# Four feed-forward weight units: the low part by a VectorE subtraction in place of an accumulating load

## The chip, the cores and the metric

The kernel runs on one core of one Trainium2 chip. The metric is the device time of one execution in microseconds. Its engines are TensorE (PE; PEld is its weight load), VectorE (DVE), ScalarE (ACT), GpSimd (POOL) and SyncE (SP), which only issues transfers here.

## The reference

The reference is a trunk of two decoder layers on 512 positions of width 1024, in float32. Layer 0 mixes tokens with a gated linear recurrence (RG-LRU), layer 1 with gated linear attention; each mixer is followed by a gated feed-forward block with a causal convolution of width 3. Every block stands between two RMS norms, scaled, shifted and gated by columns that a matrix makes from a conditioning vector. Cut to what matters here:

```
def conv_ffn(h, w_up, conv_w, conv_b, w_down):
    u = causal_dwconv(h @ w_up, conv_w, conv_b)
    g, val = jnp.split(u, 2, axis=-1)
    return (jax.nn.gelu(g) * val) @ w_down
...
        x = x + gt_m * rmsnorm(y, norm_g[i, 1])
        h = rmsnorm(x, norm_g[i, 2]) * (1.0 + sc_f) + sh_f
        y = conv_ffn(h, ffn_w_up[i], ffn_conv_w[i], ffn_conv_b[i], ffn_w_down[i])
```

In layer 0, `y` ahead of these lines is the output projection of the recurrent block. The feed-forward width is 2816, so `w_up` is 1024 x 5632.

## The kernel before, in words

**Layout.** Features lie on the 128 partitions and positions along the free dimension: `x` is 8 tiles of 128x512. Every weight matrix is cut into units of eight 128x128 blocks, 512 KB each (`unit_list`, L37), laid out in DRAM in the order of use. `("up", 0, p)` is the unit that makes 128 gate columns of layer 0's feed-forward block, `("up", 0, 22 + p)` the matching value columns.

**Split products.** A float32 matrix product is made of three products in a faster format, fp32r: high by high, high by low, low by high (`mm3`, L607). So each weight has a high part, its value rounded to fp32r by an ACT copy, and a low part, the value less the high part.

**How a unit gets there.** `load_upto` (L557) loads a unit into one of 3 `raw` buffers (SP queue, L464). ACT copies it to the high part (L438). The low part comes in one of two ways. In the ordinary way DVE subtracts the high part from `raw` (L579 and L599, recorded at L386): it needs the load and the ACT copy. Where `BYLOAD` (L480) holds, ACT writes the negated high part (L576 and L596, recorded at L433), and POOL issues a second load of the same unit from DRAM that adds to it (L469); `raw` is then free once ACT has read it twice. Most units land in one of 8 `w` slots (2048 columns, both parts); the units of `GWU` (L486), for layer 0 the pairs 1, 2 and 3, land in four general tiles `g` of 512 columns each, the high and low of two halves.

**Who comes by load.** Before the change the predicate holds for the eight units `rgg` of the recurrent block's gate branch, and for units 0, 1, 22 and 23 of `up` in layer 0: the first two pairs. Of these four, 0 and 22 lie in `w` slots (one accumulating load of 512 KB each), 1 and 23 in `g` tiles (two of 256 KB each).

**Where they are used.** `out_proj` (L746) ends the recurrent block: products of 8 output tiles, for the first half of the positions (256 columns) and then for the second; in each half the sum of squares over features (a matmul with a column of ones into a `nr` bank), its power -1/2 on POOL (L388), a broadcast matmul, then per tile a multiplication by it, the addition to `x` (both DVE), the square (ACT) and the addition to the sum (DVE); that sum goes through PE again, and `h_tile` (L732) makes the input of the feed-forward block. While this goes on for the first half, PE works on the products of the second half. The feed-forward block starts with `proj_halves` (L839) on its first seven units, 0, 22, 1, 23, 2, 24 and 3: for the first half of the positions all seven at feature tiles 0 and 1, and then each through tiles 2 to 7.

**Who sets the order.** All instructions are first recorded and then ordered by a planner (`Sched.order`, L192), a simulation with costs for each operation. It fixes one order for each engine, SP's and POOL's queues among them, and the engines then run strictly in it. PE and SP take the ready operation that was recorded first, the others the one with the longest rest of the way; DVE may wait a little for a more urgent operation (L299). The planner prices a load at its bytes by 360 KB per us and some 2 us, on one DMA stream (L323), an accumulating load at its bytes by 180 KB per us, 1.5 us ahead and 3.5 us behind (L326). What takes longer on the chip than in the plan stops the engine whose next instruction waits for it.

Of the kernel before, what the change touches and what calls it, by code (L numbers as in the profile page):

```python
# [20 lines left out]
KF = FF // P  # L21
# [455 lines left out]
                   after=after)  # L477


BYLOAD = lambda what, *i: what == 'rgg' or what == 'up' and i[0] == 0 and i[1] % KF < 2  # L480
SQ_GROUPS = ((0, 1, 2, 3, 4, 5), (6, 7))
WARM = (5, 2)
FULL = (1, 2, 2, 4)
# [13 lines left out]
def trunk(ctx, tc, xT, wall, adaT, par_d, c_d, walpha_d, ident_d, masks_d, outT):  # L497
# [56 lines left out]

    byload = {j for j, (key, _, _) in enumerate(UNITS) if BYLOAD(*key)}

# [834 lines left out]
```

## Time and profile before

| | |
|---|---|
| median of 3 runs | 1178.27 us (1177.48 to 1179.84) |
| the profiled execution's own time | 1178.37 us |
| its span, first to last instruction | 1176.6 us |
| mean granted TensorE clock | 0.996 |
| busy: DVE, ACT, POOL | 72%, 47%, 3% of the span |
| DMA | 163.68 MB, mean 139 GB/s |

The profile is one execution. Its page gives the busy time of each engine, the queues, the chain of work that ended last, and the costliest groups of instructions; other views give instructions in order of time, what an engine's idle time was ended by, and the same sums for stretches of the span. All times inside the execution are counted from the span's start. Most instructions are recorded by helpers, so one line stands for many: L386 is every DVE operation on two tensors, L399 every DVE scalar-tensor-tensor, L433 every ACT activation, L438 every ACT copy, L458 every matmul. Tiles tell them apart: `w<-raw,w` is a unit's subtraction, `g<-raw,g` that of half a unit in general tiles, `gh` are tiles of one half of the positions.

### The profile page before, as it was taken

To read this page: it belongs to the slowest core of one execution; us is meant where nothing else is said; L and a number is where in the kernel's file an instruction comes from. 1 tells how busy PE (TensorE), PEld (TensorE's weight loads), DVE (VectorE), ACT (ScalarE), POOL (GpSimd) and SP (SyncE) were. 2 spreads that over 40 slices of the span, in tenths; PEclk is the share of its full clock that TensorE was granted. 3 is DMA by queue.
4 is the path that set the end of the run, shared out by engine and by line. 5 is a ranking of instruction groups with operands and counts; after the bars stand their busy time and mean duration, and the time that the engine had idled before them with its cause. 6 is when DMAs were issued, how large, how long until landed. Compare 5 with 4: busy or idle time off the path is not lost.

```text
span 1176.6 us, 16159 instructions
## 1 busy us (share of the span) xinstructions
PE 1155.1 (98%) x6271; PEld 994.7 (85%) x6271; DVE 852.5 (72%) x1415; ACT 555.2 (47%) x878; POOL 36.8 (3%) x51
## 2 busy tenths in 40 slices
PE   7999998999999999999999999999999999999998
PEld 5876888988888888889988888899988888888887
DVE  6999977986777888766968787549745556645635
ACT  4499765544323424443578445444644333424411
POOL 0110020000000000000100000000000000000000
PEclk9999998999999999999999999999999999999999
DMA  9888593566575577531332103213143333233202
GB/s 363 280 237 272 179 280 102 162 205 209 177 231 185 183 233 232 153 113 35 112 108 90 55 18 109 72 37 108 38 160 90 108 92 106 90 105 93 72 1 72
DMA packets 47150, 163.68 MB, mean 139 GB/s; under 512 B 5121, under 2 KB 7681, under 8 KB 47074
## 3 DMA queue, kind: packets, MB, share of 16 engines
q1 hardware_dynamic: 45058, 156.36, 40.1%
q0 software_dynamic: 2016, 6.29, 3.0%
q8 instruction: 49, 0.80, 0.3%
q14 instruction: 27, 0.22, 0.1%
HBM read 160.54 MB, written 2.10 MB: 138 GB/s over the span
## 4 chain that ended last, share of the span: by engine, by line
PE 82%; ACT 7%; DVE 6%; DMA 3%; issue 1%; POOL 0%; DVEq 0%; SPq 0%; ACTq 0%; POOLq 0%
PE mm L458 80%; ACT g L433 3%; DMA raw<-in_wall_dram 3%; PE nr L458 2%; DVE g L399 2%; ACT L433 1%; DVE w L399 1%; DVE g L386 1%; ACT w L438 1%; DVE gh L386 1%; ACT w L433 1%; DVE w L386 1%; ACT g L438 1%; DVE gh L399 1%; DVE const L386 0%
## 5 line engine op out<-in xcount | busy, mean ns | idle before, releaser
L458 PE MATMUL mm<-g,w 128*128 128x512 f32 (+1 forms) x4846 | 947.1, 356 | 1.9 <-DVE g L386 0.9
L458 PEld LDWEIGHTS mm<-g,w 128*128 128x128 f32 x4846 | 803.7, 189 | 131.3 <-DVE g L386 1.6
L438 ACT CAST w<-raw 128x1024 fp32r<-128x1024 f32 x178 | 186.0, 1047 | 216.0 <-PE mm L458 203.9
L386 DVE TENSOR_TENSOR w<-raw,w 128x1024 fp32r<-128x1024 f32 (+1 forms) x168 | 203.5, 1215 | 74.1 <-ACT w L438 73.2
L399 DVE SCALAR_TENSOR_TENSOR g<-mm,const,g 128x510 f32<-128x510 f32 (+3 forms) x199 | 146.8, 747 | 97.6 <-ACT g L433 88.1
L386 DVE TENSOR_TENSOR g<-g,g 128x512 f32<-128x512 f32 (+2 forms) x213 | 126.7, 612 | 28.1 <-ACT g L438 13.3
L433 ACT ACTIVATE g<-mm,const 128x512 f32<-128x512 f32 (+1 forms) x144 | 100.9, 704 | 15.4 <-PE mm L458 15.3
L433 ACT ACTIVATE g<-g 128x512 f32<-128x512 f32 (+1 forms) x132 | 66.7, 538 | 83.3 <-DVE g L399 66.7
L458 PE MATMUL mm<-g,g 128*128 128x256 f32 (+4 forms) x716 | 98.7, 293 | 0.0
L458 PEld LDWEIGHTS mm<-g,g 128*128 128x128 f32 (+1 forms) x716 | 91.4, 191 | 4.2
L438 ACT CAST g<-g 128x512 fp32r<-128x512 f32 (+1 forms) x71 | 42.8, 608 | 107.5 <-DVE g L386 106.7
L399 DVE SCALAR_TENSOR_TENSOR araw<-araw,const 128x1024 f32<-128x1024 f32 x72 | 86.3, 1219 | 3.9 <-DMA araw<-in_adaT_dram 3.8
L386 DVE TENSOR_TENSOR g<-g,mm 128x512 f32<-128x512 f32 (+1 forms) x74 | 44.4, 612 | 42.6 <-PE mm L458 42.1
L386 DVE TENSOR_TENSOR gh<-gh,gh 128x256 f32<-128x256 f32 x97 | 40.3, 421 | 31.5 <-ACT gh L433 29.6
L458 PE MATMUL mm<-w,g 128*128 128x512 f32 x192 | 46.5, 394 | 0.2 <-ACT g L438 0.2
L390 POOL TENSOR_TENSOR sm<-sm,const 128x2 f32<-128x2 f32 (+1 forms) x19 | 18.8, 990 | 886.9 <-DVE sm L410 873.4
L458 PEld LDWEIGHTS mm<-w,g 128*128 128x128 f32 x192 | 35.4, 188 | 7.5 <-ACT g L438 0.4
L433 ACT ACTIVATE gh<-g 128x256 f32<-128x256 f32 x32 | 12.6, 413 | 48.6 <-DVE g L386 48.6
L433 ACT ACTIVATE g<-gh,const 128x256 fp32r<-128x256 f32 x48 | 22.5, 505 | 24.7 <-DVE gh L399 24.0
L399 DVE SCALAR_TENSOR_TENSOR w<-w,const 128x1024 f32<-128x1024 f32 x24 | 28.6, 1218 | 0.0
L433 ACT ACTIVATE gh<-const 128x256 f32<-128x256 f32 x48 | 18.8, 414 | 19.5 <-DVE const L386 19.3
L438 ACT COPY g<-mm 128x512 f32<-128x512 f32 (+1 forms) x39 | 21.0, 555 | 14.1 <-PE mm L458 14.0
(80 smaller groups left out, 537.5 us busy)
## 6 DMA issues: line engine op xcount, KB each, us to landing
raw<-in_wall_dram SPq DMA_DIRECT2D x192, 512.0 KB, 3.7
araw<-in_adaT_dram SPq DMA_DIRECT2D x72, 512.0 KB, 4.6
w<-in_adaT_dram SPq DMA_DIRECT2D x24, 512.0 KB, 8.0
w<-in_wall_dram POOLq DMA_DIRECT2D x10, 512.0 KB, 7.4
const<-in_xT_dram SPq DMA_DIRECT2D x4, 512.0 KB, 5.1
out_dram<-const SPq DMA_DIRECT2D x8, 256.0 KB, 2.1
g<-in_wall_dram POOLq DMA_DIRECT2D x4, 256.0 KB, 9.4
araw<-in_masks_dram SPq DMA_DIRECT2D x1, 512.0 KB, 6.3
```

Of the source, the lines that this page charges most:

```text
L386: self.s.add(eng, dur, lambda: e.tensor_tensor(out.ap(), a.ap(), b.ap(), op=op), [a, b], [out])
L390: lambda: self.nc.gpsimd.tensor_tensor(out.ap(), a.ap(), b.ap(), op=ALU.pow), [a, b], [out])
L399: return self.nc.vector.scalar_tensor_tensor(out.ap(), a.ap(), f(sc), b.ap(), op0=op0, op1=op1, **kw)
L433: return self.nc.scalar.activation(out.ap(), a.ap(), func, **kw)
L438: self.s.add("act", (0.095 if self._sb(a) else 0.052) + out.n * 0.8325e-3, lambda: self.nc.scalar.copy(out.ap(), a.ap()), [a], [out], afte ...
L458: r.append(self.nc.tensor.matmul(g[0].ap(), g[1].ap(), g[2].ap(), start=g[3], stop=g[4], **kw))
```

## The change

The predicate that names the units with accumulating loads loses its second part:

```
-BYLOAD = lambda what, *i: what == 'rgg' or what == 'up' and i[0] == 0 and i[1] % KF < 2
+BYLOAD = lambda what, *i: what == 'rgg'
```

The eight units of the gate branch are loaded as before. Units 0, 22, 1 and 23 of layer 0's feed-forward block now go through `e.tt(..., ALU.subtract)` at L579 and L599, as all other units do. The negating ACT copies and the accumulating loads of these four are not recorded any more, and the planner orders the whole program anew.

## The prediction

> **What bounds the kernel now.** I began with the page: its first lines and the DMA issues (count, KB each, us from issue to landing).
>
> ```profile
> span 1176.6 us, 16159 instructions
> PE 1155.1 (98%) x6271; PEld 994.7 (85%) x6271; DVE 852.5 (72%) x1415; ACT 555.2 (47%) x878; POOL 36.8 (3%) x51
> raw<-in_wall_dram SPq DMA_DIRECT2D x192, 512.0 KB, 3.7
> w<-in_wall_dram POOLq DMA_DIRECT2D x10, 512.0 KB, 7.4
> g<-in_wall_dram POOLq DMA_DIRECT2D x4, 256.0 KB, 9.4
> ```
>
> PE is busy for 1155.1 of 1176.6 us, so only 21.5 us can be won without taking PE work away. The ten `w` loads on POOL are the eight gate units and units 0 and 22; the four `g` loads are the halves of units 1 and 23. So 6 of 14 accumulating loads go. Next, whom PE waits for in the whole span (total, times, longest), and the chain that ended last (start, us), around the longest of these waits and after it:
>
> ```profile
> PE nr L458 <- DVE gh L386: 5.9, 1, 5.9
> PE nr L458 <- POOL sm L390: 0.6, 2, 0.3
> ```
>
> ```profile
> 163.45 14.04 DMA raw<-in_wall_dram
> 179.00 0.44 DVE gh L386
> 179.57 0.98 PE nr L458 x4
> 180.56 3.41 PE mm L458 x15
> 183.97 0.78 PE nr L458 x4
> 194.82 0.40 PE nr L458 x4
> 195.22 1.90 PE mm L458 x15
> 197.12 0.44 PE nr L458 x4
> 206.20 0.34 PE nr L458 x4
> ```
>
> ```profile
> 208.88 331.53 PE mm L458 x1632
> ```
>
> The largest wait of PE, 5.9 us, is for the first half's sum in the recurrent block's output projection, and the chain goes back from it to a raw load of 14.04 us. From 208.88 on PE has work for 331.53 us without a break, so what is won here reaches the end. Whom that wait goes back to is seen in the engines' timelines, ACT first, then DVE (the bracket is the idle time ahead):
>
> ```profile
> 168.55 0.63 ACT L433 ACTIVATE g<-raw 128x512 fp32r<-128x512 f32 x1 [2.88 <-DMA raw<-in_wall_dram]
> 177.51 1.14 ACT L438 CAST g<-raw 128x512 fp32r<-128x512 f32 x2 [2.94 <-DMA raw<-in_wall_dram]
> ```
>
> ```profile
> 165.09 0.75 DVE L386 TENSOR_TENSOR gh<-g,nr 128x256 f32<-128x256 f32 x2 [2.54 <-PE nr L458]
> 170.78 0.42 DVE L386 TENSOR_TENSOR gh<-gh,gh 128x256 f32<-128x256 f32 x1 [2.60 <-ACT gh L433]
> 179.00 1.22 DVE L386 TENSOR_TENSOR gh<-gh,gh 128x256 f32<-128x256 f32 x3 [3.45 <-ACT gh L433]
> ```
>
> ACT stands twice at the head of its queue with an instruction on a raw tile that has not landed (2.88 and 2.94 us). The squares of `x` for the norm are queued behind, and DVE, which adds them up, idles 2.60 and 3.45 us. Without these 6.05 us the sum would have been ready at 179.57 - 6.05 = 173.52. The stretches show that PE's work ran out then (columns: stretch, busy time and instructions of PE, PEld, DVE, ACT and POOL, granted clock, DMA share, GB/s):
>
> ```profile
> 156.00:165.00 9.00, 9.00 (x78) 9.00 (x77) 5.06 (x13) 7.08 (x15) 3.36 (x4) 1.00 0.78 223
> 165.00:173.68 8.68, 8.68 (x73) 8.48 (x71) 5.99 (x18) 5.80 (x16) 1.78 (x3) 1.00 1.06 277
> 173.68:179.57 5.89, 0.00 (x1) 0.03 (x1) 2.44 (x8) 2.96 (x8) 0.81 (x1) 0.84 0.79 195
> 179.57:184.75 5.18, 5.18 (x25) 5.18 (x26) 3.41 (x8) 0.55 (x2) 0.83 (x1) 0.52 0.63 176
> 184.75:197.57 12.82, 12.82 (x109) 12.82 (x109) 10.88 (x26) 7.89 (x18) 0.87 (x1) 1.00 0.18 57
> 197.57:209.00 11.43, 11.43 (x98) 11.43 (x98) 10.53 (x28) 4.91 (x11) 1.07 (x1) 1.00 0.36 124
> ```
>
> PE is idle from 173.68 to 179.57, and after that runs at 0.52 of its clock until 184.75. In the chain the same 4, 15 and 4 matmuls take 0.98, 3.41 and 0.78 us there and 0.40, 1.90 and 0.44 in the second half: 5.17 against 2.74, so the slow clock costs 2.43 us. Gap and clock are 5.89 + 2.43 = 8.32 us.
>
> Why the raw tiles are late: DMA issues in stretches of 0.2 us, at 157.38 (unit 1's load), 157.96 (the first accumulating load here) and 158.63 (unit 23's load), with us to landing:
>
> ```profile
> raw<-in_wall_dram SPq DMA_DIRECT2D x1, 512.0 KB, 3.6
> w<-in_wall_dram POOLq DMA_DIRECT2D x1, 512.0 KB, 10.4
> raw<-in_wall_dram SPq DMA_DIRECT2D x1, 512.0 KB, 9.9
> ```
>
> The load issued just ahead of the accumulating one takes 3.6 us, the one just behind it 9.9, unit 2's at 163.45 takes 14.04. The planner, whose order ACT must keep, priced an ordinary load near 3.6. While all six accumulating loads are under way the DMA engines are full (1.06 of their time at 277 GB/s from 165.00 on, against 0.78 ahead of it).
>
> **The change part by part.** The sum goes against the profiled execution: 1178.37 us, 1176.6 of it span, 0.10 above the median 1178.27 of the runs. Six negating ACT copies go (two of a whole unit, four of half a unit), and six DVE subtractions of the same sizes come. Their groups (busy, mean ns of one, idle before), the first from the whole span, the others from 150 to 215:
>
> ```profile
> L386 DVE TENSOR_TENSOR w<-raw,w 128x1024 fp32r<-128x1024 f32 x167 | 203.2, 1221 | 74.1 <-ACT w L438 73.2
> L386 DVE TENSOR_TENSOR g<-raw,g 128x512 fp32r<-128x512 f32 x7 | 4.7, 685 | 0.2 <-ACT g L438 0.2
> L433 ACT ACTIVATE g<-raw 128x512 fp32r<-128x512 f32 x4 | 2.5, 631 | 2.9 <-DMA raw<-in_wall_dram 2.9
> L433 ACT ACTIVATE w<-raw 128x1024 fp32r<-128x1024 f32 x2 | 2.1, 1056 | 0.6 <-ACT g L438 0.6
> ```
>
> ACT loses 2 x 1.056 + 4 x 0.631 = 4.6 us, and the order of ACT ahead of the squares gets shorter. ACT is 47% busy, so I cost this at nothing by itself; the cover is its own idle time, and without it the 4.6 us would be a gain.
>
> Six transfers go, 2 x 512 + 4 x 256 KB = 2 MB, with their reads and writes of the destination. That takes away what made unit 23's and unit 2's loads late. At 3.6 to 3.7 us they would have landed near 162.3 and 167.1, before ACT came to wait for them (168.55 - 2.88 = 165.67, and 177.51 - 2.94 = 174.57). Both waits gone: -5.89 us of gap, and with no gap no slow clock, -2.43.
>
> DVE gains 2 x 1.221 + 4 x 0.685 = 5.2 us. This is the price to be weighed, since DVE carries the norm. From 156 to 209 the rows add up to 38.31 us busy of 53.00. With 5.2 more it is 43.5, in a stretch that shall shrink to 53.00 - 8.32 = 44.7. Of the 14.7 us idle, 6.05 were the two waits, so 8.6 are left; if none of these could be used, DVE alone would need 38.3 + 5.2 + 8.6 = 52.1, a gain of 0.9; if all are of use, the gain is the whole 8.32. I take the upper end: 3.94 of the idle time lie between 156 and 165, ahead of the norm's DVE work, 2.54 of it in one piece waiting for PE. Units 0 and 1 have landed by then (157.38 + 3.6 = 161.0), and their subtractions, 1.22 + 2 x 0.69 = 2.6 us, fit in there. Units 22 and 23 (2.6 us) fall behind the first half's chain, where DVE waits for PE and POOL. And what the planner knows of (a subtraction in DVE's queue) it fills on PE with products of the second half; gaps come from what it doesn't know, late landings.
>
> The new wait: each subtraction waits for its load and its ACT copy, and behind it on DVE stand updates of `x`, on which PE's sum waits. The group's row gives 73.2 us of such waits over 167 subtractions, 0.44 each; for six it is 0 to 2.6 us on DVE, seldom on the path. Also raw tiles of the four units are released by DVE and not by ACT, so later loads may be issued later; that is the rival below. POOL's queue loses six issues from among the norm's powers; the wait of PE here ended on DVE and not on POOL, so this counts 0.
>
> The nearest row for the place without accumulating loads is the same transition in layer 1, where all units are subtracted by DVE: PE's row for the first half's sum, and that for the second half's broadcast.
>
> ```profile
> 792.60 0.50 PE L458 MATMUL nr<-const,gh 128*128 128x1 f32 x4
> 818.26 0.71 PE L458 MATMUL nr<-const,sm 128*128 128x128 f32 x4 [0.28 <-POOL sm L390]
> ```
>
> The sum there starts with no idle time ahead of it; only the second half's broadcast waits 0.28 us for POOL, and the row above gives such waits 0.3 us each. I take one for each half here: +0.6. **Sum:** 1178.37 - 5.89 - 2.43 + 0.60 = 1170.65, or 1170.7.
>
> A rule that speaks against the change is weighed on these powers:
>
> ```profile
> 541.03 0.69 POOL L390 TENSOR_TENSOR sm<-sm,const 128x2 f32<-128x2 f32 x1 [333.14 <-DVE sm L410]
> 574.59 1.61 POOL L390 TENSOR_TENSOR sm<-sm,const 128x2 f32<-128x2 f32 x1 [10.81 <-DVE sm L410]
> ```
>
> ```profile
> 574.43 2.35 DVE L386 TENSOR_TENSOR w<-raw,w 128x1024 fp32r<-128x1024 f32 x2
> ```
>
> The same power takes 0.69 us, or 1.61 with two subtractions beside it, 0.92 more. The Trainium skill (SBUF — State Buffer, "SBUF: two separate sides") says that a VectorE instruction with two SBUF inputs and a GpSimd one that reads SBUF exclude each other on a shared port. The trace agrees; by that rule more subtractions here hold the four powers of this stretch, with the rival that follows from it below.
>
> **The rivals.** *One wait stays* (0.15). Raw tiles are now held until DVE is through, so unit 2's or 23's load goes out later and ACT still meets one of them unlanded. For it: DVE is over 97% filled by the sum above. Price: 2.60 to 3.45 us of the gap stay; without slow clock 1178.37 - 8.32 + 3.45 = 1173.5, with it 1175.9. The Trainium skill (TensorE: Matmul & The Clock Gate, "What's actually happening") lets the clock fall after an idle window of some 3.4 us; the trace agrees for 5.89 us and shows nothing between. By it a remaining gap under that is priced by its length alone.
>
> *The powers are held* (0.05). Four times 0.92 us on the path instead of the 0.6 taken: 1170.65 + 3.68 - 0.60 = 1173.7. Against it: PE has 15 products planned between sum and broadcast, 1.90 us.
>
> *Nothing comes of it* (0.08). The loads are late for another reason: the conditioning loads go through the same engines at this time, two between 157 and 163. Then 1178.4. The 3.6 us at 157.38 speak against it. That the change does not do what it says would show as ten and four POOL loads again; the predicate leaves no room for that.
>
> *Slower: DVE falls behind* (0.10). The low parts and the first half's `h` tiles are pushed behind the second half's norm, which outranks them and holds DVE from 197.57 to 206.20, 8.63 us. If PE then has neither, it waits that long and the clock falls: 1178.37 - 8.32 + 8.63 + 2.43 = 1181.1. It decides once the 44.7 us don't hold the 43.5 plus the idle time that can't be used. Against it: PE would have all seven units at tiles 0 and 1, 42 products of 1.90/15 us, 5.3 us, and the planner sees this coming.
>
> **How the numbers follow.** The forecast has 0.62. A difference under 0.2% (2.4 us) could not be told from none here, the three runs lie 2.4 us apart. Faster: 0.62 + 0.05 + 0.10 of the first rival = 0.77; within: 0.05 of the first, 0.08, and 0.02 of the last = 0.15; slower 0.08. The range goes from all of the 8.32 with no new wait, and a run as far below its median as the lowest now (0.8), 1169.2, to the first rival with its clock, 1175.9. It holds 0.82.
>
> **What would show it.** Eight accumulating loads, none into `g`; unit 23's and 2's loads landing in 3.6 to 5 us; no ACT wait over 1 us for raw ahead of the squares; PE's wait for the sum under 0.5 us, granted clock 1.00 from 170 to 190; DVE over 90% busy from 156 to 200. Wrong would be a PE gap of 2 us or more between 160 and 215, and the releaser at its end names the rival.

## The result, and the profile after

| | median | runs |
|---|---|---|
| before | 1178.24 us | 6, 1176.69 to 1179.84 |
| after | 1172.31 us | 6, 1170.16 to 1173.24 |

The ratio is 0.9948, 95% interval 0.9936 to 0.9961: faster by 5.9 us, where 7.7 was forecast. The profiled execution of after took 1171.38 us, against 1178.37 before, 6.99 less. The page's first lines and its POOL loads:

```profile
span 1169.6 us, 16145 instructions
PE 1153.2 (99%) x6271; PEld 992.7 (85%) x6271; DVE 856.7 (73%) x1421; ACT 551.7 (47%) x872; POOL 31.6 (3%) x45
w<-in_wall_dram POOLq DMA_DIRECT2D x8, 512.0 KB, 7.2
```

DVE has six instructions more and ACT six fewer; eight accumulating loads are left and none goes into `g`. Whom PE waits for between 150 and 215 us, and the same three sums as before in the chain that ended last (start, us):

```profile
PE nr L458 <- DVE gh L399: 0.2, 1, 0.2
```

```profile
174.13 0.58 PE nr L458 x4
186.58 0.58 PE nr L458 x4
198.12 0.34 PE nr L458 x4
```

The wait of 5.9 us is gone; the first half's sum starts at 174.13 and not at 179.57, the last sum of the second half at 198.12 and not at 206.20. What made room for it is seen in the timelines of ACT and of DVE, and in the issue of unit 23's load (at 162.02, us to landing last):

```profile
166.84 0.62 ACT L438 CAST g<-raw 128x512 fp32r<-128x512 f32 x1 [0.50 <-DMA raw<-in_wall_dram]
```

```profile
173.56 1.22 DVE L386 TENSOR_TENSOR gh<-gh,gh 128x256 f32<-128x256 f32 x3 [0.46 <-DVE gh L386]
```

```profile
raw<-in_wall_dram SPq DMA_DIRECT2D x1, 512.0 KB, 4.8
```

The load lands in 4.8 us where it took 9.9; it was issued 3.4 us later than before. One wait of ACT for a raw tile is left ahead of the squares, 0.50 us, and DVE adds up the squares without the idle pieces of 2.60 and 3.45 us. The same six stretches as before (busy time of PE, PEld, DVE, ACT, POOL; granted clock; DMA share; GB/s):

```profile
156.00:165.00 9.00, 8.97 (x76) 8.79 (x75) 7.82 (x16) 4.98 (x11) 0.71 (x1) 1.00 0.74 244
165.00:173.68 8.68, 8.68 (x75) 8.68 (x74) 8.12 (x25) 6.65 (x17) 0.00 (x0) 1.00 0.34 115
173.68:179.57 5.89, 5.75 (x49) 5.58 (x48) 5.58 (x13) 1.92 (x5) 0.81 (x1) 1.00 0.23 67
179.57:184.75 5.18, 5.18 (x45) 5.18 (x45) 4.71 (x12) 3.90 (x11) 0.00 (x0) 1.00 0.36 130
184.75:197.57 12.82, 12.64 (x106) 12.47 (x106) 12.61 (x35) 7.80 (x19) 0.87 (x1) 1.00 0.35 124
197.57:209.00 11.43, 11.43 (x98) 11.43 (x97) 10.64 (x24) 5.43 (x10) 1.07 (x1) 1.00 0.26 93
```

PE works 5.75 of the 5.89 us in which it had stood still, the clock stays at 1.00, and from 165.00 on the DMA share is 0.34 and not 1.06. DVE is now nearly full: 49.49 of 53.00 us, against 38.31 (in before it takes 45.11 us from 156 to 216, which reaches as far in the work).

The gain arises in this place alone. Counting matmuls in the order of PE, number 750 ends 0.66 us later than before (at 166 us), number 1000 ends 7.00 us earlier (at 205 us), and the end of the span is 6.98 us earlier.

### The profile page after: what moved, and what is told of

The parts are those of the page before. It is cut to its first block, busy times and chain, and to the rows that moved or that the text cites. A ratio compares the mean times of both kernels' runs of the same rounds, so it can differ in the third digit from the quotient of the medians.

```text
span 1169.6 us, 16145 instructions
## 1 busy us (share of the span) xinstructions
PE 1153.2 (99%) x6271; PEld 992.7 (85%) x6271; DVE 856.7 (73%) x1421; ACT 551.7 (47%) x872; POOL 31.6 (3%) x45
## 4 chain that ended last, share of the span: by engine, by line
PE 80%; DVE 8%; ACT 7%; DMA 3%; issue 2%; POOL 0%; DVEq 0%; SPq 0%; ACTq 0%; POOLq 0%
PE mm L458 78%; ACT g L433 3%; DMA raw<-in_wall_dram 2%; PE nr L458 2%; DVE g L399 2%; ACT L433 1%; DVE w L399 1%; DVE gh L386 1%; DVE w L386 1%; DVE g L386 1%; ACT w L438 1%; ACT w L433 1%; DVE const L386 1%; DVE gh L399 1%; ACT g L438 0%
## 5 line engine op out<-in xcount | busy, mean ns | idle before, releaser
L386 DVE TENSOR_TENSOR w<-raw,w 128x1024 fp32r<-128x1024 f32 x170 | 205.8, 1215 | 72.1 <-ACT w L438 71.3
```

Source lines behind the costliest of these rows:

```text
L386: self.s.add(eng, dur, lambda: e.tensor_tensor(out.ap(), a.ap(), b.ap(), op=op), [a, b], [out])
```

## The experiments

Two theories stood after the result. The **late loads**: accumulating loads made two raw loads land later than the plan had them, and ACT, bound to its order, stood at the head of its queue while the squares waited behind. The rival, **ACT's own work**: the negating copies filled ACT ahead of the squares. A third question is whether the transfers do the harm by themselves, or only through a plan that counted on early landings. The runs were taken in three sets, each on one chip beside runs of before: e1, e4, e6 and e7 (before at 1178.70 us), e2, e3, e7b and e11 (1179.04), e8, e9, e12 and e13 (1177.69).

**The transfers go, ACT's work stays** (e1, an edit of before). ACT still writes the negated high part, and DVE adds `raw` to it:

```
-  e.accum(lo[:], wall[j, :, i * S:(i + 1) * S], P * S * 4)
+  e.tt(lo[:], part, lo[:].f32(), ALU.add)
...
-  e.accum(w[D:D + n], wall[j, :, :n], P * n * 4)
+  if UNITS[j][0][0] == 'up':
+      e.tt(w[D:D + n], raw[0:n], w[D:D + n].f32(), ALU.add)
+  else:
+      e.accum(w[D:D + n], wall[j, :, :n], P * n * 4)
```

> The kernel before, but for units 0, 22, 1 and 23 the accumulating load is replaced by a DVE addition of the raw tile to the negated high part that ACT still writes. ACT keeps its 4.6 us of negating copies, the six transfers go, DVE has the six operations of the kernel after. Theory (the accumulating transfers make the ordinary loads behind them late, and ACT waits for these at the head of its queue): as the kernel after, 1172 us within 1.5, no PE wait over 0.5 us between 160 and 200. Rival (it is ACT's own work ahead of the squares of x): the wait of PE stays for the larger part, 1176 to 1178 us.

Measured: 1171.97 us (1171.58 to 1173.73) beside 1178.70, ratio 0.9942 (0.9930 to 0.9955). The stretch in which PE stood still before:

```profile
173.68:179.57 5.89, 5.89 (x51) 5.84 (x50) 5.22 (x13) 1.61 (x5) 0.81 (x1) 1.00 0.18 40
```

PE is busy for all of it, with all of ACT's extra copies still there. The whole gain comes without taking them away, so ACT's own work was not the cause. Nor did both loads simply land earlier: unit 23's, issued at 162.73, took 5.7 us and landed at 168.44, in before at 168.53. ACT meets it without a wait, because in the new order the copy of unit 22 and two squares stand ahead of unit 23's first copy, which in before stood ahead of them:

```profile
166.93 1.05 ACT L438 CAST w<-raw 128x1024 fp32r<-128x1024 f32 x1
167.87 0.73 ACT L433 ACTIVATE gh<-const 128x256 f32<-128x256 f32 x2
168.49 0.63 ACT L433 ACTIVATE g<-raw 128x512 fp32r<-128x512 f32 x1
```

**The transfers stay, the plan prices them higher** (e4, an edit of before). Only the planner's figure for the accumulating loads of the four units changes, from 180 to 120 KB per us:

```
-    def accum(self, out, src, nbytes):
+    def accum(self, out, src, nbytes, rate=180e3):
...
-                   xfer=nbytes / 180e3)
+                   xfer=nbytes / rate)
...
-  e.accum(lo[:], wall[j, :, i * S:(i + 1) * S], P * S * 4)
+  e.accum(lo[:], wall[j, :, i * S:(i + 1) * S], P * S * 4, 120e3)
...
-  e.accum(w[D:D + n], wall[j, :, :n], P * n * 4)
+  e.accum(w[D:D + n], wall[j, :, :n], P * n * 4, 120e3 if UNITS[j][0][0] == 'up' else 180e3)
```

> The kernel before with all its accumulating loads; only the planner prices those of the four feed-forward units at 120 KB per us instead of 180, which is what the six took together in the trace (some 17 us of the DMA engines' time for 2 MB). The transfers stay as slow as they are; the plan knows of it. Theory with its second half (the loss is an order that counted on early landings): ACT's copies move behind the squares, PE's wait shrinks to under 1.5 us, the clock stays, 1171 to 1174 us. Rival (the transfers themselves, in whatever order, hold up the start of the feed-forward block): 1176.5 us or more.

Measured: 1171.23 us (1170.47 to 1172.31), ratio 0.9934 (0.9922 to 0.9947). All six transfers are there and about as slow as before (8.0 to 11.2 us from issue to landing, against 7.6 to 12.0). One accumulating load and the raw load issued at 159.15, then the last square of the first half and the copy behind it on ACT, then the two stretches around the old gap:

```profile
w<-in_wall_dram POOLq DMA_DIRECT2D x1, 512.0 KB, 9.0
raw<-in_wall_dram SPq DMA_DIRECT2D x1, 512.0 KB, 8.6
```

```profile
172.71 0.42 ACT L433 ACTIVATE gh<-const 128x256 f32<-128x256 f32 x1
176.21 1.14 ACT L438 CAST g<-raw 128x512 fp32r<-128x512 f32 x2 [1.91 <-DMA raw<-in_wall_dram]
```

```profile
165.00:173.68 8.68, 8.68 (x75) 8.68 (x75) 7.96 (x24) 8.25 (x21) 2.75 (x4) 1.00 1.07 311
173.68:179.57 5.89, 5.89 (x53) 5.89 (x52) 5.58 (x14) 2.98 (x7) 0.82 (x1) 1.00 1.07 267
```

The DMA engines are as full as before (1.07), the next raw loads take 11.8 and 8.8 us, and ACT still waits 1.91 us for one. But that copy now stands behind the squares, and PE has no gap. So slow transfers do hardly any harm here by themselves: the loss was an order that counted on early landings, in which a waiting copy held back the squares behind it. The price makes the planner order every engine anew, and no run changes ACT's order alone; that it is ACT's order is read from these rows.

The same kernel, run again on one chip with the kernel after (e12, e13):

> The priced kernel once more (the kernel before, its accumulating loads of the feed-forward units priced at 120 KB per us), beside the kernel after on one chip. Theory (the order is the cause, not the transfers): no slower than the kernel after, 1171 to 1172 us, with loads of 8 us and more that nobody waits for. Rival (its first result was the luck of one chip): 1173.5 us or more.

> The kernel after, unchanged: 1172 to 1173.5 us. Where a single execution is longer, unit 23's load should have taken over 6 us instead of under 5 and ACT waited 2 us for it.

Measured: priced 1170.88 us (1170.51 to 1171.69), ratio 0.9947 (0.9928 to 0.9966); after 1171.90 (1171.55 to 1174.34), ratio 0.9955 (0.9941 to 0.9969). The intervals overlap; the prices alone give at least about as much as the change, and which of the two is better is not settled. That nobody would wait for the slow loads was too much: in the profile of e12 ACT waits 3.0 and 1.1 us for raw tiles, and PE 0.6 us for the sum.

Three of the 18 executions of before in this set took 1172.06 to 1172.43 us, with a mean granted clock of 0.999, as short as those of after; of the 45 executions of before in the result and in the other two sets none took less than 1176.69. None of the three was profiled. They suggest that the order of before can run without its loss when the loads happen to land early; that is not shown.

**Zeros by load behind each subtraction** (e6, an edit of after). The six accumulating loads come back, but add zeros from the padding of a gate unit to a finished low part:

```
+    gz = UIDX[("gz",)]
...
+    def zeros(j, lo, n):
+        what, *i = UNITS[j][0]
+        if what == 'up' and i[0] == 0 and i[1] % KF < 2:
+            e.accum(lo, wall[gz, :, P:P + n], P * n * 4)
...
+                    zeros(j, lo[:], S)
...
+                zeros(j, w[D:D + 7 * P], 7 * P)
```

> The kernel after, and behind each of the six new subtractions an accumulating load of as many zeros into the low part (7/8 as many for the two whole units). The traffic is that of the kernel before, the ACT copies are those of the kernel after. Theory: ordinary loads that go out behind these take 8 us or more again and ACT or DVE stands for them; 1175 to 1179 us. Rival (ACT's negating copies were the cause): as the kernel after, 1171 to 1173.5.

Measured: 1173.76 us (1172.90 to 1174.29), ratio 0.9954 (0.9941 to 0.9966), below what was expected, and by another way: the transfers went out later than in before, unit 23's raw load, issued just ahead of the first of them, took 6.0 us, and ACT waited 0.4 us for a raw tile. What cost time in its profile was a power on POOL, with DVE's subtractions and PE's broadcast beside it:

```profile
189.96 1.88 DVE L386 TENSOR_TENSOR g<-raw,g 128x512 fp32r<-128x512 f32 x3
```

```profile
190.13 2.29 POOL L390 TENSOR_TENSOR sm<-sm,const 128x2 f32<-128x2 f32 x1 [9.85 <-DVE sm L410]
```

```profile
192.47 0.71 PE L458 MATMUL nr<-const,sm 128*128 128x128 f32 x4 [0.96 <-POOL sm L390]
```

The power took 2.29 us beside three subtractions and PE waited 0.96 us for it: the rival of the held powers, in another kernel. It agrees with the exclusion that the prediction took from the Trainium skill (SBUF — State Buffer, "SBUF: two separate sides"). Between the theories this run doesn't decide.

**Half of it: two units by load** (e2: units 0 and 22; e3: units 1 and 23; edits of after, with after beside them as e11).

```
-BYLOAD = lambda what, *i: what == 'rgg'
+BYLOAD = lambda what, *i: what == 'rgg' or what == 'up' and i[0] == 0 and i[1] % KF < 1
```

In e3 the end is `== 1`.

> The kernel after, unchanged, on the chip of the next three, and to stand beside the priced kernel in another measurement: 1172.3 us, a ratio of 0.995 to the kernel before.

> Only the two whole units 0 and 22 come by accumulating load (two of 512 KB), 1 and 23 by subtraction: half the bytes of the kernel before. Theory (what counts is the chip's delay of the loads behind these beyond the plan's price, met by ACT ahead of the squares): part of the wait comes back, a PE gap of 1 to 4 us between 170 and 182, 1173 to 1177 us. Rival (only the four half transfers matter): 1172 us, no gap.

> Only units 1 and 23 come by accumulating load (four of 256 KB), 0 and 22 by subtraction. Theory: as with the other half, a PE gap of 1 to 4 us, 1173 to 1177 us, and the two halves' losses against the kernel after add up to about 6 us. Rival (only the two whole transfers matter): 1172 us, no gap.

| | us | ratio to before (1179.04) |
|---|---|---|
| e11, after | 1173.56 (1171.68 to 1174.52) | 0.9952 (0.9939 to 0.9966) |
| e2, units 0 and 22 | 1177.30 (1176.51 to 1178.88) | 0.9986 (0.9977 to 0.9994) |
| e3, units 1 and 23 | 1174.41 (1171.36 to 1176.32) | 0.9963 (0.9949 to 0.9977) |

Against after, one pair costs 3.7 and the other 0.9, together 4.6 of the 5.5 us between before and after on this chip, where about 6 was expected. In both profiles the wait for the first half's sum is back, shorter. Its row in e2, and the two windows of the clock around it:

```profile
176.09 0.58 PE L458 MATMUL nr<-const,gh 128*128 128x1 f32 x4 [2.45 <-DVE gh L386]
```

```profile
174.46:177.87 3.41, 1.78 (x15) 1.81 (x16) 2.51 (x8) 2.69 (x7) 0.82 (x1) 1.00 0.01 2
177.87:181.29 3.42, 3.42 (x18) 3.42 (x18) 2.15 (x4) 0.03 (x1) 0.00 (x0) 0.50 0.37 102
```

A gap of 2.45 us was enough for the slow clock. e3's profile shows a gap of 1.99 us and the slow clock as well (0.50 from 178.27 to 181.69). But that execution took 1175.99 us, the second longest of seven, with the lowest mean clock of them, 0.997; the other six have 0.999, so the slow clock is no part of e3's median.

Nor does all of the loss arise here. At matmul 1000 the profile of e2 is 4.0 us behind that of e11, and e3's 2.5 us. In both, 1.8 us more are lost in layer 1, at a broadcast that waits for a power on POOL; in e2:

```profile
690.11 1.16 PE L458 MATMUL nr<-const,sm 128*128 128x128 f32 x8 [1.52 <-POOL sm L390]
```

The power takes 3.33 us there and 1.12 in after, with the same DVE instructions beside it; what held it was not found. So the two differences of the medians can't be put down to the transfers near 160 to 180 us alone.

e11, the kernel after itself, has a wait too in this execution, and so has e13: unit 23's load took 6.5 and 6.4 us and not 4.8. ACT and PE in e13, and the clock's windows:

```profile
168.32 0.62 ACT L438 CAST g<-raw 128x512 fp32r<-128x512 f32 x1 [2.16 <-DMA raw<-in_wall_dram]
```

```profile
175.25 0.58 PE L458 MATMUL nr<-const,gh 128*128 128x1 f32 x4 [1.44 <-DVE gh L386]
```

```profile
171.92:175.34 3.42, 1.98 (x17) 1.80 (x17) 2.86 (x9) 2.13 (x7) 0.00 (x0) 1.00 0.00 0
175.34:178.75 3.41, 3.41 (x30) 3.41 (x31) 3.27 (x8) 0.00 (x0) 0.81 (x1) 1.00 0.01 2
```

So the rival of one remaining wait is met in two profiled executions of after, at 1.4 to 1.5 us and with the clock kept.

**The clock by itself** (e7, e7b; edits of before). Filler matmuls whose results nobody reads are put ahead of the first half's sum, 20 in e7 and 38 in e7b, so that the gap is not idle and only the waiting remains:

```
+        for _ in range(0 if warm is None else 20):
+            e.mms([(nr[256:512], onesr[:], ..., True, True)], warm)
```

> The kernel before, with 20 matmuls of 256 columns of ones into an unused part of the norm's bank ahead of the first half's sum of x squared, released by the update of the seventh tile of x, so that they run in PE's gap. They add nothing to the output. Theory (2.43 us of the loss are the halved clock that follows the idle time): the sum comes when it came before, the granted clock stays at 1.00, 1175.8 us, 2.4 below the kernel before. Rival (the clock falls for another reason, or the matmuls only move the gap): 1178 us or more.

> The kernel before with 38 of the filling matmuls in place of 20, some 4.7 us, so that hardly any of PE's gap is idle. Theory (2.4 us of the loss are the halved clock, and PE has to work through most of a window of 3.4 us to keep it): granted clock 1.00 throughout 170 to 190, the sum no later than in the kernel before, 1176.3 us. Rival (the clock falls for another reason): a half clock again, 1178.5 us or more.

Measured: e7 1179.96 us (1175.85 to 1181.49), ratio 1.0008 (0.9997 to 1.0019); e7b 1181.63 (1180.16 to 1182.97), ratio 1.0020 (1.0011 to 1.0029). Both missed. In e7 the clock's windows show why:

```profile
174.96:178.37 3.41, 1.34 (x12) 1.14 (x11) 0.88 (x3) 1.81 (x4) 0.00 (x0) 1.00 1.08 261
178.37:181.78 3.41, 3.26 (x15) 3.26 (x16) 3.21 (x8) 0.17 (x2) 1.22 (x1) 0.50 0.91 236
```

PE worked 1.34 of 3.41 us, and the clock was halved all the same. In e7b it was kept through the sum, and the 15 products behind it took 2.04 us against 3.55 in e7; then a new wait followed:

```profile
179.16 2.04 PE L458 MATMUL mm<-g,w 128*128 128x256 f32 x15
183.22 1.17 PE L458 MATMUL nr<-const,sm 128*128 128x128 f32 x4 [2.03 <-POOL sm L390]
```

The scalar step on DVE ahead of the power stood behind two operations on the conditioning columns, and the clock was halved behind that wait (183.3 to 186.7). So the slow clock's price shows in the matmuls' durations, but as a part of the time it was not isolated. The single executions don't settle it either: in e7 the three with a mean clock of 0.999 took 1175.85 to 1178.18 us and the five with 0.996 or 0.997 took 1179.96 to 1181.49, but in e7b the five with 1.000 took 1180.25 to 1182.97 and the five with 0.997 or 0.998 took 1180.77 to 1182.60.

**Other ends of the same choice** (e9, e8). e9 is e4 with the gate units priced at 120 KB per us too; e8 is after with no accumulating load at all (`BYLOAD = lambda what, *i: False`).

> The priced kernel with the eight gate units' accumulating loads priced at 120 KB per us too. Theory: the first 135 us are bound by DVE and ACT and not by these loads, so nothing is won over the priced kernel, 1170.5 to 1172.5 us. Rival (raw loads of 7 to 8 us in that stretch cost time as well): 1169 us or less.

> The kernel after with no accumulating loads at all: the eight gate units are subtracted by DVE as well, 9.8 us more work of DVE in the first 135 us. Theory (what such a load is good for is a stretch in which DVE sets the pace): 1177 to 1182 us, the first 135 us longer by 5 to 10 us. Rival (these loads delay others as much as they save): 1172 us or less.

Measured beside 1177.69: e9 1186.24 us (1185.99 to 1187.24), ratio 1.0077 (1.0057 to 1.0096), some 14 above the range that was expected; e8 1181.38 (1180.12 to 1183.11), ratio 1.0042 (1.0027 to 1.0058), within it, but not in the expected place: against after, the first 131 us (500 matmuls) grew by only 0.8. PE in e9, at its longest new waits:

```profile
142.98 0.80 PE L458 MATMUL mm<-g,w 128*128 128x512 f32 x1 [2.79 <-ACT g L438]
196.04 0.58 PE L458 MATMUL mm<-g,w 128*128 128x256 f32 x1 [3.06 <-ACT g L433]
```

The price of the gate units' loads is all that e9 changes against e4, so it is the new order that costs the time, in two places, each with a spell of slow clock (142.4 to 149.2 and 193.6 to 200.4 us): e9 is 6.2 us behind e4 at matmul 600 and 15.5 at matmul 1000. Why the order comes out worse was not found. In e8 the work of DVE in the first 131 us tells where the time went, its subtractions and its conditioning columns (`araw`), first in after and then in e8:

```profile
L386 DVE TENSOR_TENSOR w<-raw,w 128x1024 fp32r<-128x1024 f32 x10 | 12.2, 1218 | 2.9 <-ACT w L438 2.9
L399 DVE SCALAR_TENSOR_TENSOR araw<-araw,const 128x1024 f32<-128x1024 f32 x8 | 9.6, 1212 | 0.0
```

```profile
L386 DVE TENSOR_TENSOR w<-raw,w 128x1024 fp32r<-128x1024 f32 x17 | 20.7, 1220 | 4.5 <-ACT w L438 4.5
L399 DVE SCALAR_TENSOR_TENSOR araw<-araw,const 128x1024 f32<-128x1024 f32 x3 | 3.6, 1218 | 0.0
```

Seven subtractions more are done there and five column operations fewer; these come later, beside the norm. DVE, ACT and PE at that place in e8:

```profile
187.63 1.22 DVE L399 SCALAR_TENSOR_TENSOR araw<-araw,const 128x1024 f32<-128x1024 f32 x1
```

```profile
189.09 2.36 ACT L433 ACTIVATE g<-gh,const 128x256 fp32r<-128x256 f32 x5 [4.13 <-DVE const L386]
```

```profile
189.65 1.95 PE L458 MATMUL mm<-g,w 128*128 128x256 f32 x6 [5.47 <-ACT g L433]
```

A column that `h` needs is made only at 187.63, `h` follows, PE waits 5.47 us and then runs at half clock. Up to matmul 850 (180 us) e8 is 0.7 us behind after, at matmul 950 (202 us) 9.9, and that stays to the end. This is the rival "DVE falls behind", in a kernel with eight more subtractions (8 x 1.22 = 9.8 us) than the one after.

## Why the prediction was right

**The gap (-5.89).** Right in size, and in that both of ACT's waits go: the sum waits 0.2 us at most in the profile after, and units 23's and 2's loads land in 4.8 and 4.97 us, in the range given. But the step that was to bring this about is not what the trace shows. The prediction let the loads go out as before and land near 162.3 and 167.1, ahead of 165.67 and 174.57, when ACT had come to wait. DVE now holds the raw buffers, so unit 23's load goes out at 162.02 and not at 158.63, and lands at 166.82; unit 2's goes out at 178.11, as the chain shows:

```profile
178.11 4.97 DMA raw<-in_wall_dram
```

Both land later than the times named. ACT stands for them only 0.50 us ahead of the squares, since in the new plan the copy of unit 22 comes before unit 23's and all squares of the first half come before unit 2's. The planner computes when a buffer comes free, so it knew of these late loads; it had not known of those in before.

That ACT's 4.6 us count nothing by themselves is shown by e1. What the prediction took as one cause is two: the accumulating loads made others late, and the plan didn't know it. e1 and e4 agree that the second decides.

**The slow clock (-2.43).** Right in the profile, where the granted clock is 1.00 in all six stretches. As a time of its own it was not shown (e7, e7b).

**DVE takes 5.2 us (0).** Right. From 165.00 to 173.68 it works 8.12 us where it had 5.99, and the sum isn't late for it. There is no slack, though: PE's products end at 173.98 and the sum starts at 174.13.

**Two POOL waits (+0.60).** This is the term that was mis-sized, in place and amount. None came in the stretch; the four powers take 0.71 to 1.07 us, nothing waits for them. In their place 0.66 us are lost ahead of matmul 750, of which PE's waits between 131 and 166 us explain 0.3 to 0.4: 1.2 and 0.4 us, against 0.9 and 0.3. From there to matmul 1000 the shift is 7.66, not 8.32, and of this 0.66 some 0.3 are pieces in which PE isn't busy (0.14 in the stretch from 173.68, 0.18 in that from 184.75). The rest of both, about 0.6 us, is not assigned. So the profile has -6.99 where the sum had -7.72.

**From the profile to the median.** The medians differ by 5.93, the profiled executions by 6.99. The prediction's execution of before stood near its median; that of after is among its faster ones. In e11 and e13 the late landing of unit 23 leaves a wait of 1.4 to 1.5 us, but these executions took 1171.68 and 1172.50 us, so that wait does not give the whole spread of after, up to 1174.5. What the slower executions do is not seen in any profile.

**The rivals.** *One wait stays* holds in part, as told, at about half the price and without the slow clock. Its reason holds for unit 23, whose load goes out 3.4 us later and is met unlanded in e11 and e13. Unit 2's goes out late too, at 178.11 and not at 163.45, but ACT has no copy of it ahead of the squares any more, and it costs nothing. *The powers are held* happened in e6, not in after. *DVE falls behind* happened in e8; in after DVE was nearly full and nothing that PE needed came late. *Nothing comes of it* is excluded by every run of after (0.9948, 0.9952, 0.9955). One statement was wrong: that a remaining gap under 3.4 us is priced by its length alone. In e2 2.45 us of gap brought the slow clock.

## What to carry to other kernels

When an engine that keeps a fixed order stands idle at the head of its queue, look at what the plan believed of the awaited transfer before taking the transfer away: here a price alone (e4) gave what the change gave. A price that is right for one stretch must be tried over the whole program, since the same edit made everywhere cost 0.8% (e9). And work that is moved to a nearly full engine (DVE was 86% busy in the first 131 us of after) is safe only as long as nothing is pushed behind it that the critical path needs next: 9.8 us more of such work, moved far ahead of the critical place, cost 9.9 us there, by a wait of PE and the slow clock behind it (e8).

## What was not expected of the hardware

**The clock counts in windows.** Inside each trace the changes of the granted clock lie whole multiples of 3.41 us apart (in before at 177.71, 184.54 and 1174.40 us, two and 290 such steps). Between 170 and 190 us a window in which PE was busy for 0.39 (1.34 of 3.41, e7), 0.40 (1.38, e7b) or 0.52 of it (1.78, e2 and e3) was followed by one at half clock; after 0.58 (1.98 of 3.42, e13) the clock was kept. So a gap of 2.0 to 2.5 us within one window cost the clock here, and a gap of 1.4 us didn't. The busy share alone doesn't set the bound, however: the last products of e7 fill 0.46 of a window, and the clock is kept behind it:

```profile
1171.65:1175.06 3.41, 1.56 (x8) 1.05 (x6) 2.83 (x8) 1.57 (x5) 0.00 (x0) 1.00 0.42 148
1175.06:1178.17 3.11, 0.00 (x0) 0.00 (x0) 0.00 (x0) 0.00 (x0) 0.00 (x0) 1.00 0.50 175
```

Where the bound lies is not shown. The Trainium skill (TensorE: Matmul & The Clock Gate, "What's actually happening") has the clock fall after a window that is idle; the windows of 0.39 to 0.52 weren't, and the measurement decides.

**Accumulating transfers occupy the engines about twice as long.** The rows of the two queues on the page of after, ordinary loads first (packets, MB, share of 16 engines' span):

```profile
q1 hardware_dynamic: 45058, 156.36, 40.1%
q0 software_dynamic: 1152, 4.19, 2.1%
```

That is 0.26% of the span for each MB of ordinary loads and 0.50% for the accumulating ones, and in before and e4 the ordinary loads of 512 KB issued from 158 to 173 us, beside them, took 8.6 to 14 us to land, where those of after in that stretch took 4.8 to 5.0.
